# A hybrid decoder layer on one core: SiLU as one ScalarE function, taken for four convolution tiles at a time

## The chip, the core and the metric

The kernel runs on one core of a Trainium2 chip. A core has five engines, each working through its own queue of instructions in order: TensorE (PE; its weight loads are listed as PEld) multiplies matrices, VectorE (DVE) and ScalarE (ACT) work element by element, GpSimd (POOL) does so more slowly, and SyncE (SP) issues most DMAs. Engines wait for each other through semaphores. The metric is the time of one execution on the device in microseconds (us): the median of three runs, and beside it one execution that the hardware profiler recorded.

## The reference, cut to what matters

One layer of a decoder with three token mixers runs over 256 prompt rows and 8 x 4 sample rows, 288 columns in all, in fp32. The part that the change touches is the front of mixer B, a gated delta rule with 4 heads of width 128:

```python
conv = sum(full[:, j:j + L] * conv_w[j] for j in range(CONV_W))      # width 4, per channel
conv = jax.nn.silu(conv).astype(jnp.float32).reshape(n, L, 3, B_HEADS, B_HEAD_DIM)
q = l2_normalize(conv[:, :, 0]) * (B_HEAD_DIM ** -0.5)
k = l2_normalize(conv[:, :, 1])                  # x * rsqrt(sum(x * x) + 1e-6)
v = conv[:, :, 2]
...
o = rms_norm(o, dn_g) * jax.nn.silu(b_z.astype(jnp.float32).reshape(n, L, B_HEADS, B_HEAD_DIM))
```

So 12 channel tiles of 128 (4 of q, 4 of k, 4 of v) are convolved and put through SiLU; q and k are normalised over their 128 channels; four z tiles go through SiLU for the output gate. Around this stand the projections in and out, two attention mixers, the residual norms and an MLP with squared ReLU.

## The kernel before, in words

**Pieces.** All weights come as a list of pieces of 128 x 1024 or 128 x 768, and the main loop in `build` walks through them. A weight is split into a high part (`wh`, a cast on ScalarE, L372) and a low part (`wl`, a subtraction on VectorE, or on GpSimd for a few pieces), the activations likewise (`xh`, `xl`), and each product is three matmuls: high x high, low x high, high x low. A piece of 8 tiles is 24 matmuls, one of 6 tiles is 18. `split_to(i + SA)` with SA = 3 emits the cast of a piece three pieces ahead, into four buffers; `low_to` emits its low part one piece later. Pieces 0 to 88 are the input projection (`w_in`): the attention heads first, then z, a small piece for the gates, and as pieces 65 to 88 the 12 tiles of b, two pieces each. Pieces 89 to 120 are the first output projection (`w_o1`), 121 to 128 the second (`w_o2`), then the MLP.

**Planned side work.** All other work is written as Python generators whose `yield` gives a latency in us of a planning clock `clk`, which counts only estimated TensorE time. Between parts of a piece `advance(BUD)` steps each generator that is ready, in the order of the list, until 1.6 us of planned TensorE work are emitted; `drain(name)` forces a generator to its end. This fixes the order of the instructions in every engine's queue before the program runs; nothing is reordered later.

**The convolution stage.** When both pieces of b tile m are through, `conv_tile(m)` scales the accumulator into `zb` with the rows that precede it, and adds a generator `g_conv(m)` ahead of the others. `g_conv` makes the convolution from one ScalarE and three VectorE instructions (`ca`), then SiLU in parts that need only Exp and Ln: a clamp on VectorE, `silu_e` (Exp, Ln, Exp on ScalarE), `silu_b` (two steps on VectorE, the product on GpSimd). For q and k it goes on: the square (ScalarE), the sum over channels (a matmul with ones), Ln and Exp for a first inverse root `r`, its square, two VectorE steps for the refinement, a product with `r` on GpSimd, and a last product on GpSimd that writes `B["q"]` or `B["k"]` (for the 32 sample columns two small ones into `qD`, `kD`). For v it ends with transposes into `B["vt"]`. Waits in the code keep at most three tiles apart. `g_silu_z` does the same SiLU for the four z tiles when all 12 convolutions are through.

**What follows.** `g_gate` prepares decays early in the stage. `g_chunk(0)` and `g_chunk(1)`, the delta rule of the prompt, poll until the tiles 0 to 7 are done, and need 8 to 11 later; `g_bdec` handles the sample rows and needs the buffers that open when the convolution pool `cv` closes; `g_bfin` applies norm and gate once all are done. The last `w_o1` piece drains `bc0`, `bc1` and `bf`, since `w_o2` reads their result. Later norms (`pre_up`, `g_r2`, the end of the loop) each take Ln and Exp on ScalarE through `rsqrt_a`. At its start the kernel asks for one table of ScalarE functions by name:

```python
S.preload_act_table_set("natural_log_exp_and_others")
```

Helpers record all their uses under one line: `act` is L314, `tt` L317, `ts` L321 and L323, `stt` L326, `mm` L307, `tr` L311.

Of the kernel before, what the change touches and what calls it, by code (L numbers as in the profile page):

```python
# [7 lines left out]
AF = mybir.ActivationFunctionType  # L8
ALU = mybir.AluOpType
# [4 lines left out]
P = 128  # L14
# [3 lines left out]
T = TP + TS  # L18
# [3 lines left out]
EPS = 1e-6  # L22
ZW = 315
CW = 312
# [215 lines left out]
def build(tc, d):  # L240
    nc = tc.nc
    PE, V, S, G, SP = nc.tensor, nc.vector, nc.scalar, nc.gpsimd, nc.sync
# [23 lines left out]
    def mx(n=512, p=P):  # L266
        return ps.t([P, 512], "mx", 4)[0:p, 0:n]
# [6 lines left out]
    ident, ones, tri, triD = (cst[:, k * P:(k + 1) * P] for k in range(4))  # L274
# [10 lines left out]
    dng = pm[:, 112:113]  # L285
# [23 lines left out]
    def tr(out, in_, idn):  # L309
        clk[0] += max(in_.shape[0], in_.free_size()) / 600.0  # L310
        PE.transpose(out, in_, idn)  # L311

    def act(out, in_, func, **kw):
        S.activation(out=out, in_=in_, func=func, **kw)  # L314

    def tt(eng, out, a, b, op):
        eng.tensor_tensor(out=out, in0=a, in1=b, op=op)  # L317

    def ts(eng, out, a, s1, op0, s2=None, op1=None):
        if op1 is None:  # L320
            eng.tensor_scalar(out=out, in0=a, scalar1=s1, scalar2=None, op0=op0)  # L321
        else:
            eng.tensor_scalar(out=out, in0=a, scalar1=s1, scalar2=s2, op0=op0, op1=op1)  # L323

    def stt(eng, out, a, s, b, op0, op1, **kw):
        eng.scalar_tensor_tensor(out=out, in0=a, scalar=s, in1=b, op0=op0, op1=op1, **kw)  # L326
# [23 lines left out]
    LT = (2.8, 2.8, 3.6, 1.4, 1.4, 2.8, 1.4, 1.4, 5.0)  # L350
# [88 lines left out]
    done = set()  # L439

    def add_gen(g, name=None, lat=0.0, front=False):
        at_ = len(gens)
        if front:
            at_ = sum(1 for x in gens if x[1].startswith("conv") and x[1] != "convout")
        gens.insert(at_, (g, name, clk[0] + lat))
# [41 lines left out]
    def drain(*names):  # L487
        guard = 0
        while any(n not in done for n in names):
            for name in [g[1] for g in sorted(gens, key=lambda g: g[2])]:  # L490
                if guard % 6 < 5 and name not in names:
                    continue
                for i in range(len(gens)):
                    if gens[i][1] == name:
                        step(i)
                        break
                if all(n in done for n in names):
                    return
            guard += 1
            assert guard < 5000, (names, [g[1] for g in gens])  # L500
# [8 lines left out]
    mixp = base.t([P, KT, T], "mix")  # L509
# [16 lines left out]
    bp, cv, sp, st = Lazy(), Lazy(), Lazy(), Lazy()  # L526
    cvp = {}
    gate = {}
    B = {}

    def open_b():
        bp.open("b", "right")
        cv.open("cv")
        cvp["buf"] = cv.t([P, 12, 24], "cbuf")
        cvp["co"] = cv.t([P, 12, 27], "convo")
        SP.dma_start(out=cvp["buf"], in_=d["cbuf"])
        B["k"], B["q"] = (bp.t([P, 4, TP], "k4", 2) for _ in range(2))
        B["vt"] = bp.t([P, 2, 4, P], "vt")
        B["kD"], B["qD"], B["vD"] = (bp.t([P, P], t) for t in ("kD", "qD", "vD"))
        B["o"] = bp.t([P, 4, T], "oB")  # L540
        add_gen(g_silu_z(), "siluz", 6.0)
        add_gen(g_gate(), "gate")
        for c in range(2):
            add_gen(g_chunk(c), f"bc{c}")
        add_gen(g_bdec(), "bd")
        add_gen(g_bfin(), "bf")

    def g_silu_z():
        for h in range(4):
            z = mixp[:, 6 + h, :]  # L550
            while not all(f"cs{m}" in done for m in range(12)):
                yield 3.0
            e, q = silu_a(cv, z, T)
            yield 2.0
            silu_e(e, q)
            yield 4.0
            silu_b(e, q, z, G)
            yield 2.5
            act(z, z, AF.Identity, scale=dng)
            yield 1.0  # L560

    def maybe_close_cv():
        if "sp" not in done and all(n in done for n in ["siluz", "gate", "convout"] + [f"conv{m}" for m in range(12)]):
# [2 lines left out]
            sp.open("sp")  # L566
            done.add("sp")

    def silu_a(pool, x, w):
        e = pool.t([P, ZW], "e", 3)  # L570
        s = pool.t([P, ZW], "s", 3)
        ts(V, e[:, :w], x, -80.0, ALU.max)
        return e[:, :w], s[:, :w]

    def silu_e(e, s):
        act(e, e, AF.Exp, scale=-1.0)
        act(s, e, AF.Ln, bias=1.0, scale=1.0)
        act(s, s, AF.Exp, scale=-1.0)

    def silu_b(e, s, x, eng):  # L580
        stt(V, e, e, 1.0, s, ALU.add, ALU.mult)
        stt(V, s, e, 2.0, s, ALU.subtract, ALU.mult, reverse0=True)
        tt(eng, x, x, s, ALU.mult)

    def decv(ap):
        return ap[:, 259:315].rearrange("p (n s) -> p n s", s=7)[:, :, 0:4]

    def conv_tile(m, acc):
        if m >= 4:
            drain(f"conv{m - 4}")  # L590
        if m >= 3:
            drain(f"cz{m - 3}")
        zb = cv.t([P, ZW], "zb", 3)
        G.memset(zb[:, 0:3], 0.0)
        zd = zb[:, 259:315].rearrange("p (n s) -> p n s", s=7)
        G.tensor_copy(out=zd[:, :, 0:3], in_=cvp['buf'][:, m, :].rearrange("p (n s) -> p n s", s=3))
        R = cur["R"]
        tt(V, zb[:, 3:259], acc[:, 0:TP], R[:, 0:TP], ALU.mult)
        tt(V, zd[:, :, 3:7], acc[:, TP:T].rearrange("p (n s) -> p n s", s=4),
           R[:, TP:T].rearrange("p (n s) -> p n s", s=4), ALU.mult)  # L600
        G.tensor_copy(out=cvp['co'][:, m, 0:3], in_=zb[:, 256:259])
        G.tensor_copy(out=cvp['co'][:, m, 3:27].rearrange("p (n s) -> p n s", s=3), in_=zd[:, :, 4:7])
        add_gen(g_conv(m, zb), f"conv{m}", 1.5, front=True)
        if m == 11:
            add_gen(g_convout(), "convout")

    def g_convout():
# [2 lines left out]
            yield 2.0  # L610
        G.dma_start(out=d["conv"], in_=cvp['co'])

    def g_conv(m, zb):
        kind, h = m // 4, m % 4
        while m >= 3 and f"cs{m - 3}" not in done:
            yield 1.0
        y = cv.t([P, ZW], "ca", 5)
        yc = y[:, :CW]
        act(yc, zb[:, 0:CW], AF.Identity, scale=convw[:, m, 0:1])
        yield LT[6]  # L620
        for j in range(1, 4):
            stt(V, yc, zb[:, j:j + CW], convw[:, m, j:j + 1], yc, ALU.mult, ALU.add)
        e = cv.t([P, ZW], "e", 3)[:, :CW]
        q = cv.t([P, ZW], "s", 3)[:, :CW]
        ts(V, e, yc, -80.0, ALU.max)
        done.add(f"cz{m}")
        yield LT[0]
        silu_e(e, q)
        yield LT[1]
        silu_b(e, q, yc, G)  # L630
        done.add(f"cs{m}")
        yield LT[2] if kind < 2 else LT[8]
        if kind < 2:
            while m >= 2 and f"cn{m - 2}" not in done:
                yield 1.0
            sq = cv.t([P, ZW], "sq", 2)
            act(sq[:, :CW], yc, AF.Square)
            yield LT[3]
            p = lx(CW)
            mm(p, ones, sq[:, :CW])  # L640
            yield LT[4]
            r = cv.t([P, CW], "nr", 2)
            act(r, p, AF.Ln, bias=epsc[:, 0:1], scale=1.0)
            act(r, r, AF.Exp, scale=-0.5)
            w = sq[:, :CW]
            act(w, r, AF.Square)
            yield LT[5]
            sc = float(P) ** -0.5 if kind == 0 else 1.0
            stt(V, w, p, EPS, w, ALU.add, ALU.mult)
            ts(V, w, w, -0.5 * sc, ALU.mult, 1.5 * sc, ALU.add)  # L650
            tt(G, yc, yc, r, ALU.mult)
            yield LT[7]
            dp, dd = ((B["q"], B["qD"]), (B["k"], B["kD"]))[kind]
            tt(G, dp[:, h, :], y[:, 0:TP], w[:, 0:TP], ALU.mult)
            yv = decv(y)
            dv_ = dd[:, 32 * h:32 * h + 32].rearrange("p (n s) -> p n s", s=4)
            tt(G, dv_[:, 0:7, :], yv[:, 0:7, :], sq[:, 259:308].rearrange("p (n s) -> p n s", s=7)[:, :, 0:4], ALU.mult)
            tt(G, dv_[:, 7, :], yv[:, 7, :], sq[:, 308:312], ALU.mult)
            done.add(f"cn{m}")
        else:  # L660
            G.tensor_copy(out=B["vD"][:, 32 * h:32 * h + 32].rearrange("p (n s) -> p n s", s=4), in_=decv(y))
            p = mx(256)
            for c in range(2):
                tr(p[:, c * P:(c + 1) * P], y[:, c * P:(c + 1) * P], ident)
            S.copy(out=B["vt"][:, :, h, :], in_=p.rearrange("p (c n) -> p c n", c=2))

    def g_gate():
        pool = bp
# [972 lines left out]
    with tc.manual_schedule():  # L1641
# [90 lines left out]
        p = mx(T)  # L1732
        mm(p, ones, ml["acc"], stop=False)
        mm(p, ones, ml["sql"], start=False)
        t, r = rsqrt_a(ml["p"], p, 1.0 / D, "m")
        newton(V, r, t, p, r, 1.0 / D, EPS)
        y = ml["y"]
# [35 lines left out]
```

## Time and profile before

| | us |
|---|---|
| median of three runs (lowest, highest) | 1449.59 (1447.74, 1450.51) |
| the profiled execution | 1447.53 |
| its span | 1445.8 |
| busy: TensorE, VectorE, ScalarE, GpSimd | 1391.1, 826.5, 605.6, 212.2 |

The span runs from the first to the last instruction; some 2 us of the execution's time lie around it. A group's row names line, engine and operation, output <- inputs with their pool's name (`cv` is the convolution stage's pool, `b` the delta rule's, `sp` the output gate's, `ml` the MLP's, `base` what lives throughout, `ps` the accumulators), partitions x elements, the count, and then the busy time and the mean of one instruction. A timeline row begins with the start and the duration in us, and in brackets stands the idle time of its engine before it with what ended it. TensorE's busy time comes from modelled ends of pipelined matmuls, so the granted clock (PEclk) has to be read beside it.

### The profile page before, as it was taken

What the parts mean: (1) busy time and instruction counts of PE and PEld (TensorE: products, weight loads), DVE (VectorE), ACT (ScalarE), POOL (GpSimd) and SP (SyncE); (2) the same over time, 40 slices, a digit from 0 to 9 for tenths busy, and PEclk for the clock granted to TensorE, in tenths of its full rate; (3) what the DMA queues carried; (4) which work ended last, traced back from release to release, by engine and by line L of the source; (5) the groups of instructions that cost most, each with busy time, mean ns of one, the idle gap of its engine ahead of it and who ended that gap; (6) DMA issues with size and microseconds to landing.
All of it is one profiled execution on the core that took longest, in us unless ns stands there. A gap on an engine that the chain in (4) does not pass through costs nothing.

```text
span 1445.8 us, 25828 instructions
## 1 busy us (share of the span) xinstructions
PE 1391.1 (96%) x10673; PEld 1322.8 (91%) x10673; DVE 826.5 (57%) x1310; ACT 605.6 (42%) x958; POOL 212.2 (15%) x266
## 2 busy tenths in 40 slices
PE   7899999999999999899999999999999999999994
PEld 7788788789889999699999999999999999999994
DVE  7354455547998657895533455544555444555555
ACT  6342434435664236553333334333334333334441
POOL 2112110104851015620000000000000000000114
PEclk9999999999999999999999999999999999999997
DMA  7778888743333335365545445545545545445541
GB/s 265 262 267 321 314 309 337 279 166 124 129 103 104 107 125 168 131 198 181 171 166 168 154 160 175 164 160 172 163 160 174 167 159 171 164 158 174 169 153 65
DMA packets 70629, 262.26 MB, mean 181 GB/s; under 512 B 8080, under 2 KB 10256, under 8 KB 70512
## 3 DMA queue, kind: packets, MB, share of 16 engines
q1 hardware_dynamic: 68112, 254.94, 51.5%
q0 software_dynamic: 1536, 4.89, 0.9%
q8 instruction: 83, 1.36, 0.4%
q10 hardware_dynamic: 864, 0.80, 0.2%
q14 instruction: 34, 0.28, 0.1%
HBM read 253.35 MB, written 7.24 MB: 180 GB/s over the span
## 4 chain that ended last, share of the span: by engine, by line
PE 84%; DVE 9%; issue 2%; ACT 2%; DMA 1%; POOL 1%; SPq 0%; POOLq 0%; DVEq 0%; ACTq 0%
PE ps_mx L307 33%; PE ps_acc L307 31%; PE ps_lx L307 20%; DVE cv_ca L326 2%; DVE base_wl L317 2%; PE ps_mx L311 1%; POOL ml_y L317 1%; DMA kv_kv<-kv_k 1%; DVE base_mix L317 1%; DMA base_wr<-w_in 1%; DVE base_xl L326 1%; ACT base_wh L372 1%; DVE cv_e L326 0%; DVE base_xl L317 0%; DVE ml_sacc L317 0%
## 5 line engine op out<-in xcount | busy, mean ns | idle before, releaser
L372 ACT CAST base_wh<-base_wr 128x1024 fp32r<-128x1024 f32 (+1 forms) x384 | 395.2, 1031 | 579.5 <-PE ps_mx L307 221.9
L317 DVE TENSOR_TENSOR base_wl<-base_wr,base_wh 128x1024 fp32r<-128x1024 f32 (+1 forms) x377 | 462.9, 1242 | 67.1 <-ACT base_wh L372 65.3
L307 PE MATMUL ps_acc<-base_xh,base_wh 128*128 128x288 f32 (+1 forms) x1072 | 331.4, 310 | 5.0 <-ACT base_xh L1449 2.8
L307 PE MATMUL ps_acc<-base_xl,base_wh 128*128 128x288 f32 (+1 forms) x1072 | 321.5, 300 | 3.2 <-DVE base_xl L326 3.1
L307 PE MATMUL ps_acc<-base_xh,base_wl 128*128 128x288 f32 x1056 | 315.1, 298 | 0.6 <-DVE base_wl L317 0.6
L307 PEld LDWEIGHTS ps_acc<-base_xh,base_wh 128*128 128x128 f32 (+1 forms) x1072 | 203.9, 190 | 25.6 <-issue 16.8
L307 PEld LDWEIGHTS ps_acc<-base_xl,base_wh 128*128 128x128 f32 (+1 forms) x1072 | 203.9, 190 | 7.7 <-DVE base_xl L326 6.1
L307 PEld LDWEIGHTS ps_acc<-base_xh,base_wl 128*128 128x128 f32 x1056 | 202.6, 192 | 1.5 <-DVE base_wl L317 1.4
L307 PE MATMUL ps_mx<-ml_big,base_wh 128*128 128x288 f32 x1024 | 203.3, 294 | 0.0
L307 PEld LDWEIGHTS ps_mx<-ml_big,base_wh 128*128 128x128 f32 x1024 | 164.1, 188 | 0.0
L307 PE MATMUL ps_mx<-base_xh,base_wh 128*128 128x288 f32 x512 | 151.7, 296 | 1.1 <-DVE st_s L317 1.1
L307 PE MATMUL ps_mx<-base_xh,base_wl 128*128 128x288 f32 x512 | 150.8, 295 | 0.5 <-DVE base_wl L317 0.4
L307 PE MATMUL ps_mx<-base_xl,base_wh 128*128 128x288 f32 x512 | 151.0, 295 | 0.0
L307 PE MATMUL ps_mx<-ml_big,base_wl 128*128 128x288 f32 x512 | 150.9, 295 | 0.0
L307 PE MATMUL ps_lx<-base_xh,base_wh 128*128 128x288 f32 x416 | 126.0, 303 | 6.3 <-ACT base_xh L314 6.3
L317 POOL TENSOR_TENSOR ml_sacc<-ml_sacc,ml_sq 128x288 f32<-128x288 f32 x20 | 18.3, 913 | 742.9 <-ACT ml_sq L314 742.8
L307 PE MATMUL ps_lx<-base_xh,base_wl 128*128 128x288 f32 x416 | 123.3, 296 | 1.6 <-DVE base_wl L317 1.6
L307 PE MATMUL ps_lx<-base_xl,base_wh 128*128 128x288 f32 x416 | 123.6, 297 | 0.0
L307 PE MATMUL ps_lx<-ml_big,base_wh 128*128 128x288 f32 x512 | 101.8, 294 | 0.0
L307 PE MATMUL ps_acc<-ml_big,base_wh 128*128 128x288 f32 x512 | 101.8, 294 | 0.0
L307 PEld LDWEIGHTS ps_mx<-base_xh,base_wh 128*128 128x128 f32 x512 | 95.9, 187 | 1.7 <-ACT ml_sq L314 1.0
L307 PEld LDWEIGHTS ps_mx<-base_xh,base_wl 128*128 128x128 f32 x512 | 96.4, 188 | 1.0 <-DVE base_wl L317 0.9
(392 smaller groups left out, 1993.8 us busy)
## 6 DMA issues: line engine op xcount, KB each, us to landing
base_wr<-w_up SPq DMA_DIRECT2D x128, 512.0 KB, 3.7
base_wr<-w_dn SPq DMA_DIRECT2D x128, 512.0 KB, 3.4
base_wr<-w_in SPq DMA_DIRECT2D x88, 512.0 KB, 4.4
kv_kv<-kv_k SPq DMA_DIRECT2D x24, 896.0 KB, 8.4
kv_kv<-kv_v SPq DMA_DIRECT2D x28, 768.0 KB, 7.8
base_wr<-w_o SPq DMA_DIRECT2D x32, 384.0 KB, 3.0
base_wr<-w_o SPq DMA_DIRECT2D x8, 512.0 KB, 3.5
ml_big<-xT SPq DMA_DIRECT2D x4, 576.0 KB, 5.4
```

The lines of the kernel that those rows point to most:

```text
L307: PE.matmul(out, lhsT=lhsT, rhs=rhs, start=start, stop=stop, **kw)
L311: PE.transpose(out, in_, idn)
L317: eng.tensor_tensor(out=out, in0=a, in1=b, op=op)
L326: eng.scalar_tensor_tensor(out=out, in0=a, scalar=s, in1=b, op0=op0, op1=op1, **kw)
L372: S.copy(out=p["wh"], in_=p["wr"])
```

## The change

`g_conv` now ends after the convolution itself. The generator `g_group(kind)`, one for q, k and v each, waits until its four tiles are convolved, then emits four ScalarE SiLU instructions in a row. The group of q first also takes SiLU over the four z tiles as one instruction 1152 wide, and scales them with `dng`; `g_silu_z`, `silu_a`, `silu_e` and `silu_b` are gone. After that the group walks through its tiles one by one. The norm's square of `r` on ScalarE and its scale-and-shift on VectorE are replaced by two further VectorE steps that multiply by `r` each time, so that the whole factor is in `w`, and the product with `r` on GpSimd is gone: one product with `w` remains for the prompt columns (and the two small ones). The convolved tiles live in nine buffers where there were five. The names of functions and tables elsewhere are as before.

```diff
-        add_gen(g_silu_z(), "siluz", 6.0)
...
     def conv_tile(m, acc):
-        if m >= 4:
-            drain(f"conv{m - 4}")
+        if m >= NCA:
+            while f"conv{m - NCA}" not in done:
+                drain(f"convg{(m - NCA) // 4}")
...
-        add_gen(g_conv(m, zb), f"conv{m}", 1.5, front=True)
+        add_gen(g_conv(m, zb), f"convt{m}", 1.5, front=True)
+        if m % 4 == 3:
+            add_gen(g_group(m // 4), f"convg{m // 4}", 1.5, front=True)
...
+    NCA = 9
+
     def g_conv(m, zb):
-        kind, h = m // 4, m % 4
-        while m >= 3 and f"cs{m - 3}" not in done:
-            yield 1.0
-        y = cv.t([P, ZW], "ca", 5)
+        y = cv.t([P, ZW], "ca", NCA)
+        cvp["y", m] = y
...
-        e = cv.t([P, ZW], "e", 3)[:, :CW]
-        q = cv.t([P, ZW], "s", 3)[:, :CW]
-        ts(V, e, yc, -80.0, ALU.max)
         done.add(f"cz{m}")
-        yield LT[0]
-        silu_e(e, q)
-        yield LT[1]
-        silu_b(e, q, yc, G)
-        done.add(f"cs{m}")
...
+    def g_group(kind):
+        ms = range(4 * kind, 4 * kind + 4)
+        while not all(f"cz{m}" in done for m in ms):
+            yield 1.0
+        yield 1.5
+        if kind == 0:
+            zs = mixp[:, 6:10, :]
+            act(zs, zs, AF.Silu)
+        for m in ms:
+            yc = cvp["y", m][:, :CW]
+            act(yc, yc, AF.Silu)
+        if kind == 0:
+            act(zs, zs, AF.Identity, scale=dng)
+            done.add("siluz")
+        yield 2.0
+        for m in ms:
+            h = m % 4
+            y = cvp.pop(("y", m))
+            yc = y[:, :CW]
+            if kind == 2:
...
+                done.add(f"conv{m}")
+                yield 0.7
+                continue
             sq = cv.t([P, ZW], "sq", 2)
             act(sq[:, :CW], yc, AF.Square)
-            yield LT[3]
+            yield 1.0
             p = lx(CW)
             mm(p, ones, sq[:, :CW])
-            yield LT[4]
+            yield 1.0
             r = cv.t([P, CW], "nr", 2)
             act(r, p, AF.Ln, bias=epsc[:, 0:1], scale=1.0)
             act(r, r, AF.Exp, scale=-0.5)
             w = sq[:, :CW]
-            act(w, r, AF.Square)
-            yield LT[5]
             sc = float(P) ** -0.5 if kind == 0 else 1.0
-            stt(V, w, p, EPS, w, ALU.add, ALU.mult)
-            ts(V, w, w, -0.5 * sc, ALU.mult, 1.5 * sc, ALU.add)
-            tt(G, yc, yc, r, ALU.mult)
-            yield LT[7]
+            stt(V, w, p, EPS, r, ALU.add, ALU.mult)
+            stt(V, w, w, -0.5 * sc, r, ALU.mult, ALU.mult)
+            stt(V, w, w, 1.5 * sc, r, ALU.add, ALU.mult)
+            yield 2.0
```

More of the change, by code (lines that the diff above doesn't have):

```diff
@@ L546, in open_b @@
         add_gen(g_bfin(), "bf")
[L548 to L554, printed above, removed]
-            silu_e(e, q)
[L556 to L559, printed above, removed]
-            yield 1.0
     def maybe_close_cv():
@@ L567, in maybe_close_cv @@
             done.add("sp")
[L569 to L583, printed above, removed]
     def decv(ap):
@@ L611, in g_convout @@
         G.dma_start(out=d["conv"], in_=cvp['co'])
+    NCA = 9
     def g_conv(m, zb):
-        kind, h = m // 4, m % 4
-        while m >= 3 and f"cs{m - 3}" not in done:
-            yield 1.0
-        y = cv.t([P, ZW], "ca", 5)
+        y = cv.t([P, ZW], "ca", NCA)
+        cvp["y", m] = y
         yc = y[:, :CW]
@@ L622, in g_conv @@
             stt(V, yc, zb[:, j:j + CW], convw[:, m, j:j + 1], yc, ALU.mult, ALU.add)
-        e = cv.t([P, ZW], "e", 3)[:, :CW]
-        q = cv.t([P, ZW], "s", 3)[:, :CW]
-        ts(V, e, yc, -80.0, ALU.max)
         done.add(f"cz{m}")
-        yield LT[0]
-        silu_e(e, q)
-        yield LT[1]
-        silu_b(e, q, yc, G)
-        done.add(f"cs{m}")
[L632 to L635, printed above, removed]
+    def g_group(kind):
[18 more added lines that the diff above has]
+            if kind == 2:
+                G.tensor_copy(out=B["vD"][:, 32 * h:32 * h + 32].rearrange("p (n s) -> p n s", s=4), in_=decv(y))
+                p = mx(256)
+                for c in range(2):
+                    tr(p[:, c * P:(c + 1) * P], y[:, c * P:(c + 1) * P], ident)
+                S.copy(out=B["vt"][:, :, h, :], in_=p.rearrange("p (c n) -> p c n", c=2))
+                done.add(f"conv{m}")
+                yield 0.7
+                continue
             sq = cv.t([P, ZW], "sq", 2)
             act(sq[:, :CW], yc, AF.Square)
-            yield LT[3]
+            yield 1.0
             p = lx(CW)
             mm(p, ones, sq[:, :CW])
-            yield LT[4]
+            yield 1.0
             r = cv.t([P, CW], "nr", 2)
@@ L658, in g_conv @@
             tt(G, dv_[:, 7, :], yv[:, 7, :], sq[:, 308:312], ALU.mult)
[L659 to L665, printed above, removed]
+            done.add(f"conv{m}")
     def g_gate():
```

## The prediction

> **What bounds the kernel now.** First the page: TensorE is busy 96% of the span, so only stretches in which it waits or runs at a lower clock can give time back. The table of stretches (us from the span's start; busy time and instructions of each engine, granted clock, DMA) shows one around the change:
>
> ```profile
> core 0: us, PE busy (x) PEld busy (x) DVE busy (x) ACT busy (x) POOL busy (x), PEclk, DMA share, GB/s
> 330.00:346.00 16.00, 14.57 (x105) 13.60 (x105) 13.55 (x24) 7.96 (x14) 5.92 (x13) 1.00 0.42 140
> 346.00:362.00 16.00, 15.86 (x104) 15.33 (x104) 13.58 (x29) 10.80 (x22) 8.25 (x15) 0.89 0.34 115
> 362.00:423.00 61.00, 55.30 (x392) 53.71 (x391) 59.74 (x90) 42.06 (x82) 48.04 (x69) 0.97 0.35 115
> 423.00:445.00 22.00, 19.88 (x146) 18.24 (x145) 21.62 (x49) 14.23 (x34) 7.24 (x10) 1.00 0.30 98
> ```
>
> From 362 to 423, VectorE is busy 59.7 of 61 us, TensorE 55.3. TensorE's idle time in the four rows is 1.4 + 0.1 + 5.7 + 2.1 = 9.4 us; the clock costs about 0.11 x 15.9 + 0.03 x 55.3 = 3.4 us more. So 12.8 us is the most that this stage can give: 3.3 before 362, 7.4 to 423, 2.1 behind. The chain of waits, cut to this stage, agrees, and the same chain later gives TensorE's own rate, 25.60 / 192 = 0.133 us a matmul:
>
> ```profile
> by line: DVE cv_ca L326 20.3%; DVE base_wl L317 12.2%; PE ps_acc L307 11.8%; issue 8.3%; DVE cv_e L326 5.4%; PE ps_mx L307 4.0%; DVE base_xl L317 3.9%; DVE cv_s L326 3.4%; PE ps_lx L307 3.3%; ACT base_wh L372 3.2%; DVE cv_zb L317 2.9%; ACT
> ...
> 673.24 25.60 PE ps_mx L307 x192
> ```
>
> Two tiles are four weight pieces, 96 matmuls: 12.8 us, and about 1 us for two norm sums: 13.8. What two tiles take now is the step from one row to the next but one of its kind in VectorE's timeline:
>
> ```profile
> 379.23 4.18 DVE L326 SCALAR_TENSOR_TENSOR cv_ca<-cv_zb,base_pm,cv_ca 128x312 f32<-128x312 f32 x3
> ...
> 395.79 4.19 DVE L326 SCALAR_TENSOR_TENSOR cv_ca<-cv_zb,base_pm,cv_ca 128x312 f32<-128x312 f32 x3
> ...
> 412.35 2.18 DVE L326 SCALAR_TENSOR_TENSOR cv_ca<-cv_zb,base_pm,cv_ca 128x312 f32<-128x312 f32 x3
> ...
> 430.98 1.70 DVE L326 SCALAR_TENSOR_TENSOR cv_ca<-cv_zb,base_pm,cv_ca 128x312 f32<-128x312 f32 x3
> ```
>
> That is 16.56 us for a pair. The same three instructions take 1.70 us where GpSimd is quiet, 2.18 beside one GpSimd product and 4.19 beside GpSimd's low part of a weight piece: GpSimd's work costs VectorE time.
>
> **The change, part by part.** The groups of instructions between 330 and 445 (x count | busy us, mean ns):
>
> ```profile
> L372 ACT CAST base_wh<-base_wr 128x1024 fp32r<-128x1024 f32 (+1 forms) x29 | 28.1, 968 | 9.5 <-PE ps_acc L307 9.5
> L326 DVE SCALAR_TENSOR_TENSOR cv_e<-cv_e,cv_s 128x312 f32<-128x312 f32 x12 | 9.5, 791 | 0.0
> L323 DVE TENSOR_SCALAR cv_sq<-cv_sq 128x312 f32<-128x312 f32 x8 | 6.5, 810 | 0.3
> L314 ACT ACTIVATE cv_s<-cv_s 128x312 f32<-128x312 f32 (+1 forms) x13 | 6.0, 463 | 0.4
> L326 DVE SCALAR_TENSOR_TENSOR cv_s<-cv_e,cv_s 128x312 f32<-128x312 f32 x12 | 5.8, 484 | 0.4
> L321 DVE TENSOR_SCALAR cv_e<-cv_ca 128x312 f32<-128x312 f32 x12 | 3.9, 323 | 0.4
> L326 DVE SCALAR_TENSOR_TENSOR cv_sq<-ps_lx,cv_sq 128x312 f32<-128x312 f32 x8 | 3.8, 474 | 0.0
> L314 ACT ACTIVATE cv_nr<-ps_lx,base_epsc 128x312 f32<-128x312 f32 x8 | 4.1, 513 | 0.0
> L314 ACT ACTIVATE cv_sq<-cv_nr 128x312 f32<-128x312 f32 x8 | 3.7, 466 | 0.3
> ```
>
> VectorE, for a pair of tiles: removed are the clamp, the two SiLU steps and the scale-and-shift, 2 x (0.323 + 0.791 + 0.484 + 0.810) = 4.8 us, and the stall beside GpSimd's SiLU product, 2 x 0.48 = 1.0; added are two more scalar-tensor-tensors a tile, 4 x 0.474 = 1.9. The remaining GpSimd product will push something else by about 0.5 a tile, 1.0. 16.56 - 5.8 + 1.9 + 1.0 = 13.7 us. VectorE alone would then no longer bind; TensorE's 13.8 would, and nearly all of the 7.4 us would come back.
>
> ScalarE, for a pair: now 42.06 / 61 x 16.56 = 11.4 us. Away go three functions of the SiLU and the square of the factor, 2 x (3 x 0.463 + 0.466) = 3.7; one function comes, 2 x 0.463 = 0.9. That leaves 8.6 us, but the function tables are not in it. The whole run before has one load of them:
>
> ```profile
> L1642 ACT ACT_TABLE_LOAD  x1: 1283/1283/1283, 0.7 to 0.7; - x1
> ...
> 4.62 1.04 ACT L372 CAST base_wh<-base_wr 128x1024 fp32r<-128x1024 f32 x1 [2.60 <-DMA base_wr<-w_in]
> ```
>
> The kernel asks for it by name, for the set natural_log_exp_and_others, and Exp, Ln, Square and Identity all run on it. No row shows SiLU, so its loads are bounded from both sides: none, if that set held it, or one at each change between SiLU, Ln and Exp. I take the second: the new code names no set after the first SiLU, and a load placed for Ln alone, in front of Ln alone, need not bring Exp with it. Then each of the two normalised groups has 1 + 4 x 2 = 9 loads, the third 1, the delta rule's first Exp 1, and each later Ln and Exp pair (output gate, two norms of the MLP, the last norm) 2: 28 loads, 28 x 1.283 = 36 us of ScalarE. A switch costs at least 1.283; behind the one load stand 2.60 us of idle time, so at most 3.88; but a DMA ended that idle time, so I take 1.283.
>
> A pair with two norms then has 8.6 + 4 x 1.283 + half a SiLU switch (0.6) = 14.3 us of ScalarE. The planner spaces the norms of a group by 4.0 of its own us plus rounding to its calls, about 5.6, and the tiles by 6.3, so a group's norms come 1.13 times as dense: about 15. ScalarE becomes the bound, with VectorE (13.7, and now waiting in order for each Exp) and TensorE (13.8) right behind it. I take 15.6 for a pair; between 15 and 16.6 lie gains of 5.7 and 0. 61 / 16.56 = 3.7 pairs x 0.95 = **3.5 us gained** from 362 to 423.
>
> Before 362 the pieces that were late are mostly these:
>
> ```profile
> 343.11 1.75 POOL L317 TENSOR_TENSOR cv_ca<-cv_ca,cv_s 128x312 f32<-128x312 f32 x1 [0.54 <-DVE cv_s L326]
> ...
> 345.40 0.38 PE L307 MATMUL ps_mx<-base_cst,cv_bD 8*128 8x8 f32 x2 [1.43 <-POOL cv_bD L693]
> ```
>
> TensorE waits for a copy queued on GpSimd behind the SiLU product, and the clock drops behind the wait (0.89). The product is gone, the first group's SiLU comes only after tile 3: **3 us gained** of 3.3 (0 if another wait steps in).
>
> From 423 to 445: in the old order the norms ended with the win stage; now the last two tiles' Ln and Exp (2 x 3.5 us of ScalarE) and the third SiLU switch fall beside the twelve casts of the mixer's output and the weight casts. **1 us lost** (2 gained to 4 lost). The z tiles' SiLU, moved from 441-497 into group 0, costs ScalarE 2 x 1.17 us there (a 1152 wide instruction, row below) and frees a stretch in which TensorE was full anyway: nothing, covered by the weight casts' lead of three pieces (9.6 us); without it, those 2.3 us.
>
> Behind the stage, the chunk generators start when tile 7 is done. Its yields after the tile add to 19.1 before and 22.4 now, and there are more of them to round up, and the calls thin out at the stage's end: about 3 pieces of the 32 of the first output projection later. Its end, the output gate, already comes late:
>
> ```profile
> 537.91 1.17 ACT L314 ACTIVATE sp_fa<-b_oB 128x1152 f32<-128x1152 f32 x1
> ...
> 547.14 1.19 ACT L314 ACTIVATE sp_fb<-sp_fb 128x1152 f32<-128x1152 f32 x1
> ...
> 550.71 1.68 DVE L326 SCALAR_TENSOR_TENSOR sp_ft<-sp_ft,sp_fa 128x1152 f32<-128x1152 f32 x1
> ...
> 556.08 1.34 DVE L317 TENSOR_TENSOR base_mix<-base_mix,sp_ft 128x1152 f32<-128x1152 f32 x1
> ...
> 557.94 0.61 PE L307 MATMUL ps_acc<-base_xh,base_wh 128*128 128x288 f32 x1 [2.85 <-ACT base_xh L1449]
> ```
>
> It takes 20 us from its square to TensorE's restart. Its own work is about 13: these rows with the step between the VectorE ones (1.8), a second 1.2 on ScalarE, a cast of 0.4, and some 4 for four sums and their evacuations. So 7 us are slack, of which I count 2 as weight casts that stay in between. Starting 3 pieces (3 x 18 x 0.133 = 7.2 us) later it loses 7.2 - 5 = 2.2 us, and the load ahead of its Exp 1.3: **3.5 us lost** (2 gained to 6 lost). The later norms sit bare on the path:
>
> ```profile
> 587.37 1.03 ACT L372 CAST base_wh<-base_wr 128x1024 fp32r<-128x1024 f32 x1
> 588.66 0.50 ACT L314 ACTIVATE ml_m_r<-ps_mx,base_epsc 128x288 f32<-128x288 f32 x1 [0.26 <-PE ps_mx L307]
> ...
> 1426.08 0.54 ACT L314 ACTIVATE ml_y<-ml_y,base_pm 128x288 f32<-128x288 f32 x1
> 1426.89 0.50 ACT L314 ACTIVATE ml_m_r<-ps_mx,base_epsc 128x288 f32<-128x288 f32 x1 [0.27 <-PE ps_mx L307]
> ```
>
> ScalarE is free at 588.40 and Ln starts at 588.66: a load in front delays it by 1.0, the load for Exp by 1.3; at the end likewise 0.9 + 1.3. With 0.4 for the norm between, **4.9 us lost**.
>
> Sum: 3 + 3.5 - 1 - 3.5 - 4.9 = 2.9 us slower than the profiled 1447.53; on the median of 1449.59, which lies 2.1 above it, and with half a microsecond for instructions that no longer overlap across a load: **1453 us**.
>
> By the Trainium skill, "ScalarE: Activation LUTs", What ACT_TABLE_LOAD costs, a switch costs the 1283 ns of this trace's row and a drain of about 1380 ns, 2.66 us in all. By that figure the estimate is the second rival's time. No run here shows it yet.
>
> **The rivals.** (1) After the SiLU one set serves Ln and Exp again. Then a group has two switches, 6 loads in all and none later: ScalarE has 8.6 + 1.3 us for a pair, TensorE binds; 3 + 6.5 gained, 1 lost at the stage's end, 2.2 at the gate: **1443**. For it: one load served both before. Against: that one was asked for by name. By the skill's "ScalarE activation tables", Table sets in the compiler and the runtime, loads are placed for the longest run, which gives this rival.
> (2) A switch costs about twice its load, 2.6 us. A pair then has 15 + 4.5 x 1.3 = 21 us of ScalarE: 3.7 x 4.4 = 16 lost where 3.5 was gained, some 4 more to 445, 6 at the later norms: 1453 + 30 = **1483**. For it: the idle time behind the only load; against: the DMA that ended it.
> (3) Loads as forecast, but ScalarE runs ahead and hides them in the stage, since TensorE waits there for nothing but VectorE: 7 gained of 7.4, the end of the stage even; 3 + 7 - 3.5 - 4.9 = 1.6 gained: **1448**. It decides from the point at which a pair costs ScalarE under 13.8 us.
>
> **How the numbers follow.** Forecast 0.62, its own range 1446 to 1460; (1) 0.13; (2) 0.12; (3) 0.13. A measurement of this kernel tells about 0.2%, 2.9 us, from no change. The forecast alone is slower 0.53, the same 0.35, faster 0.12; (1) is faster 0.85; (2) slower; (3) faster 0.45, same 0.5. Together faster 0.24, same 0.30, slower 0.46. The range of 1443 to 1467 leaves out (2) and the outer ends of the rest.
>
> **What would show it.** Right: 29 table loads, in Ln and Exp pairs; ScalarE over 90% busy between tiles 4 and 11, a pair near 15.6 us; TensorE's wait at 345 gone; each later norm 2.2 us longer; a longer wait at the first weight of the second output projection. Wrong: about 7 loads and a pair of 14 us (1); pairs over 20 us with idle time behind each load (2); pairs at 14 us in spite of 29 loads (3). A stage with no TensorE idle time before 445 would show that the chunk work's later start mattered more than the loads.

## The result

| | before | after |
|---|---|---|
| median (lowest, highest), us | 1449.25 (1447.74, 1450.51) | 1464.03 (1460.20, 1464.65) |
| ratio to before | | 1.010 (95% interval 1.0087 to 1.0112) |
| span of the profiled execution | 1445.8 | 1462.8 |
| busy: TensorE, VectorE, ScalarE, GpSimd | 1391.1, 826.5, 605.6, 212.2 | 1395.0, 800.5, 622.3, 183.0 |

The kernel became 15 us slower. The sign of the forecast holds, and 1464.03 lies in the range of 1443 to 1467; but it lies above the forecast's own range of 1446 to 1460, and the size does not hold, since 3.4 us were forecast. One of the ten executions of the new norm alone, below, took 1532.19 us at a granted clock of 0.842, and it is left out of that kernel's ratio.

The table of stretches of the changed kernel (us from the span's start; busy time and instructions of each engine, granted clock, DMA), for the stretches that the prediction shows of before:

```profile
core 0: us, PE busy (x) PEld busy (x) DVE busy (x) ACT busy (x) POOL busy (x), PEclk, DMA share, GB/s
330.00:346.00 16.00, 16.00 (x119) 15.16 (x117) 11.84 (x22) 6.21 (x10) 6.60 (x12) 1.00 0.38 120
346.00:362.00 16.00, 16.00 (x123) 16.00 (x123) 12.77 (x23) 9.56 (x15) 7.04 (x12) 1.00 0.47 154
362.00:423.00 61.00, 51.10 (x341) 48.33 (x339) 36.23 (x61) 47.10 (x63) 24.63 (x48) 0.94 0.34 111
423.00:445.00 22.00, 18.29 (x119) 17.06 (x120) 18.35 (x40) 18.55 (x38) 6.48 (x12) 0.84 0.24 73
```

Up to 362 TensorE no longer waits and its clock is full. Behind it, VectorE falls from 59.7 to 36.2 us of 61, GpSimd from 48.0 to 24.6, and ScalarE reaches 47.1, 77%. TensorE falls too, from 55.3 to 51.1, 84%. No engine is full. From 330 to 445 TensorE issues 119 + 123 + 341 + 119 = 702 matmuls where it issued 747: 45 x 0.133 = 6 us behind.

ScalarE's groups over the whole run, table loads alone (count | busy us, mean ns | idle before):

```profile
L314 ACT ACT_TABLE_LOAD x28 | 35.9, 1283 | 0.5
...
L1623 ACT ACT_TABLE_LOAD x1 | 1.3, 1283 | 0.7 <-PEq L1744 0.7
```

The 28 loads of the forecast are there, each as long as the one of before. ScalarE's timeline shows where they fall (start, duration; in brackets the idle time before and what ended it):

```profile
394.36 1.28 ACT L314 ACT_TABLE_LOAD   x1
395.66 1.17 ACT L314 ACTIVATE cv_ca<-cv_ca 128x312 f32<-128x312 f32 x3
399.12 0.46 ACT L314 ACTIVATE cv_ca<-cv_ca 128x312 f32<-128x312 f32 x1 [2.30 <-DVE cv_ca L326]
399.49 1.03 ACT L372 CAST base_wh<-base_wr 128x1024 fp32r<-128x1024 f32 x1
400.43 0.46 ACT L314 ACTIVATE cv_sq<-cv_ca 128x312 f32<-128x312 f32 x1
...
402.29 1.28 ACT L314 ACT_TABLE_LOAD   x1
403.58 0.52 ACT L314 ACTIVATE cv_nr<-ps_lx,base_epsc 128x312 f32<-128x312 f32 x1
404.12 1.28 ACT L314 ACT_TABLE_LOAD   x1
405.41 0.46 ACT L314 ACTIVATE cv_nr<-cv_nr 128x312 f32<-128x312 f32 x1
...
442.39 1.28 ACT L314 ACT_TABLE_LOAD   x1
443.68 1.28 ACT L314 ACTIVATE b_cA<-b_cA,b_ngc 128x128 f32<-128x128 f32 x4
```

The second group's SiLU burst waits in ScalarE's queue 2.3 us for the last of its four convolutions, and the square of tile 4 stands behind it and a weight cast. Then the norms of tiles 4 to 7 follow one another, each with a load ahead of Ln and one ahead of Exp, and only behind tile 7, the third burst and one more load comes the first Exp of the delta rule (`b_cA`), at 443.68. In the kernel before:

```profile
429.51 1.26 ACT L314 ACTIVATE b_cA<-b_cA,b_ngc 128x128 f32<-128x128 f32 x4
```

TensorE's longest waits between 330 and 650 in the changed kernel (us in total, times, longest):

```profile
PE ps_acc L307 <- ACT base_xh L1430: 9.4, 2, 7.1
PE ps_lx L307 <- ACT cv_sq L314: 8.4, 4, 6.3
```

And its timeline at the output gate, first ScalarE's square, then TensorE's first matmul behind the gate:

```profile
549.50 1.17 ACT L314 ACTIVATE sp_fa<-b_oB 128x1152 f32<-128x1152 f32 x1
...
569.02 0.61 PE L307 MATMUL ps_acc<-base_xh,base_wh 128*128 128x288 f32 x1 [7.13 <-ACT base_xh L1430]
```

The longest of the `cv_sq` waits, 6.3 us, is the sum of tile 4 waiting for the square above. The longest of all, 7.1 us, stands at the gate: its square comes at 549.50 instead of 537.91, and TensorE restarts at 569.02 instead of 557.94. The delta rule starts 14.2 us later, the gate comes 11.6 later, TensorE's restart 11.1.

Part of this lies ahead of the change. VectorE's first convolution steps, those of tile 0, in the kernel before and in the changed one:

```profile
337.35 1.70 DVE L326 SCALAR_TENSOR_TENSOR cv_ca<-cv_zb,base_pm,cv_ca 128x312 f32<-128x312 f32 x3 [0.56 <-ACT cv_ca L314]
...
339.14 1.70 DVE L326 SCALAR_TENSOR_TENSOR cv_ca<-cv_zb,base_pm,cv_ca 128x312 f32<-128x312 f32 x3 [0.56 <-ACT cv_ca L314]
```

None of the changed instructions stands ahead of this one, and two kernels below that are alike up to here (the set named in each group, and named last) reach it 2.0 us apart. So instants of two kernels are better compared from this step on. Counted so, the first Exp comes 12.4 us later, the gate's square 9.8, TensorE's restart 9.3.

### The profile page after: what moved, and what is told of

Read it like the earlier page. It is cut to its first block, busy times and chain, and to the rows that moved or that the text cites. A ratio compares the mean times of both kernels' runs of the same rounds, so it can differ in the third digit from the quotient of the medians.

```text
span 1462.8 us, 25757 instructions
## 1 busy us (share of the span) xinstructions
PE 1395.0 (95%) x10673; PEld 1324.3 (91%) x10673; DVE 800.5 (55%) x1270; ACT 622.3 (43%) x940; POOL 183.0 (13%) x242
## 4 chain that ended last, share of the span: by engine, by line
PE 64%; DVE 3%; POOL 2%; ACT 1%; issue 1%; POOLq 0%; DVEq 0%; ACTq 0%
PE ps_mx L307 31%; PE ps_lx L307 17%; PE ps_acc L307 16%; POOL ml_y L317 1%; DVE base_mix L317 1%; POOL base_R L317 1%; DVE base_xl L326 0%; ACT L314 0%; DVE ml_sacc L317 0%; DVE base_wl L317 0%; DVE base_oext L317 0%; DVE sp_ft L326 0%; PE ps_mx L311 0%; ACT sp_fb L314 0%; ACT base_wh L372 0%
## 5 line engine op out<-in xcount | busy, mean ns | idle before, releaser
L317 DVE TENSOR_TENSOR base_wl<-base_wr,base_wh 128x1024 fp32r<-128x1024 f32 (+1 forms) x377 | 460.6, 1236 | 72.1 <-ACT base_wh L372 68.5
L307 PEld LDWEIGHTS ps_acc<-base_xh,base_wh 128*128 128x128 f32 (+1 forms) x1072 | 204.0, 190 | 33.1 <-issue 17.6
```

What stands on the lines that cost most here:

```text
L307: PE.matmul(out, lhsT=lhsT, rhs=rhs, start=start, stop=stop, **kw)
```

## The experiments

Three theories were open. L: the table loads make the loss. O: the order makes it, since the groups queue much behind each SiLU burst. And, from the second set of runs on, C: what counts is how late the delta rule starts, because the gate follows its first Exp one for one, whatever delays it. None of the kernels below leaves work out.

**The named set behind each burst.** The changed kernel with one line more, so that Ln and Exp find the set that holds both:

```diff
             done.add("siluz")
+        S.preload_act_table_set("natural_log_exp_and_others")
         yield 2.0
```

> The changed kernel, with the set that has both Ln and Exp asked for by name right behind each group's SiLU instructions: 7 loads in all instead of 29. Theory L (the loads and what queues behind them cost the time): ScalarE needs some 10 us for a pair of tiles, TensorE binds again; 1445 us, within 3, so faster than before. Theory O (the later start of the chunk work, an effect of the grouping's order alone, costs most of it): only the loads at the later norms and at the output gate are saved, about 6 us; 1457 us, with the long wait ahead of the second output projection still there.

Measured: 1447.77 us, 0.9994 of before (0.9984 to 1.0004). ScalarE's groups, the loads but for the one at the start:

```profile
L314 ACT ACT_TABLE_LOAD x3 | 3.8, 1283 | 0.1
L611 ACT ACT_TABLE_LOAD x3 | 3.8, 1283 | 0.1
```

The timeline at the points shown above:

```profile
432.13 1.28 ACT L314 ACTIVATE b_cA<-b_cA,b_ngc 128x128 f32<-128x128 f32 x4
...
539.31 1.17 ACT L314 ACTIVATE sp_fa<-b_oB 128x1152 f32<-128x1152 f32 x1
...
557.45 0.61 PE L307 MATMUL ps_acc<-base_xh,base_wh 128*128 128x288 f32 x1 [5.76 <-ACT base_xh L1431]
```

Six loads in place of 28, the same order of work, and the whole loss is gone: L holds, O's 1457 does not. But nothing is won either, in a kernel that frees VectorE. The stretches say where the gain went:

```profile
362.00:423.00 61.00, 54.82 (x368) 52.26 (x366) 45.85 (x82) 38.41 (x67) 23.35 (x49) 0.94 0.35 112
423.00:445.00 22.00, 21.92 (x176) 21.92 (x177) 18.32 (x39) 15.62 (x35) 9.23 (x15) 1.00 0.43 132
```

With 119 and 122 matmuls in the two stretches ahead, TensorE issues 785 from 330 to 445, 38 or 5 us more than before. But counted from the first convolution the first Exp is 0.8 us later than before and the gate's square only 0.4 earlier. So the matmuls done ahead of time are handed back: TensorE waits 5.8 us at the gate (2.85 before), and from its restart to the row `ml_y<-ml_y,base_pm` of the last norm it takes 870.6 us (868.1 before).

**The named set only behind the last burst**, which takes the loads of the later stages away and leaves those of the stage:

```diff
             done.add("siluz")
+        if kind == 2:
+            S.preload_act_table_set("natural_log_exp_and_others")
         yield 2.0
```

> The changed kernel, with the set asked for by name only behind the third group's SiLU: the loads in the convolution stage stay (19 of them), those of the output gate, the MLP norms and the last norm go. Both theories: 2.2 us each at two later norms and 1.3 us at the gate, so 1458 us. It parts the loads of the stage from the later ones: under theory L the step from here to the run with a named set in each group is over 10 us, under theory O under 3 us.

Measured: 1456.93, 1.006 (1.0045 to 1.0075).

ScalarE's timeline:

```profile
441.47 1.28 ACT L314 ACTIVATE b_cA<-b_cA,b_ngc 128x128 f32<-128x128 f32 x4
...
547.28 1.17 ACT L314 ACTIVATE sp_fa<-b_oB 128x1152 f32<-128x1152 f32 x1
```

So the loads of the stage cost 1456.93 - 1447.77 = 9.2 us, near the 10 that L wanted and far over O's 3. Counted from the first convolution (337.18 here, 339.18 with the set named in each group), the first Exp is 11.3 us later and the gate's square 10.0. The two kernels differ by 14 loads, 18.0 us of ScalarE. The loads behind the stage are the step to the changed kernel, 1464.03 - 1456.93 = 7.1.

**The new norm alone**, in the kernel before with its own SiLU, and the reverse: the groups with the named set and the norm of before.

```diff
-            act(w, r, AF.Square)
...
-            stt(V, w, p, EPS, w, ALU.add, ALU.mult)
-            ts(V, w, w, -0.5 * sc, ALU.mult, 1.5 * sc, ALU.add)
-            tt(G, yc, yc, r, ALU.mult)
+            stt(V, w, p, EPS, r, ALU.add, ALU.mult)
+            stt(V, w, w, -0.5 * sc, r, ALU.mult, ALU.mult)
+            stt(V, w, w, 1.5 * sc, r, ALU.add, ALU.mult)
```

> The kernel before with the new norm alone (three VectorE steps that use the factor directly, no square of the factor on ScalarE, one GpSimd product less); SiLU and its order as before. VectorE by its rows: 0.810 us of scale-and-shift replaced by 2 x 0.474 a tile, and some 0.5 us less beside the GpSimd product: 0.4 us a tile gained on eight tiles, so 1447 us; if the GpSimd product cost VectorE nothing, 1450 to 1451 us.

> SiLU in groups as in the change and the table set named again behind each group, one tile at a time (1447.77), but the norm of before: square of the factor on ScalarE, one scalar-tensor-tensor and one scale-and-shift on VectorE, two GpSimd products. If the new norm is what costs here, as alone in the kernel before (2.6 us slower): 1445. If the prediction's VectorE sum is right, where the new norm frees 0.5 us of VectorE for a pair plus the stall beside the GpSimd product: 1449 to 1451. If the norm is not on the chain: 1447.8.

Measured: 1451.24 for the new norm alone, 1.0017 (1.0008 to 1.0027), and 1448.20 for the groups with the old norm, 1.000 (0.9991 to 1.0009). The stretch of the new norm alone:

```profile
362.00:423.00 61.00, 52.89 (x384) 51.32 (x383) 59.54 (x94) 37.91 (x72) 43.72 (x65) 1.00 0.37 119
```

That is the dearer of the two cases, in which the product on GpSimd costs VectorE nothing: VectorE stays at 59.5 of 61 us, and from 330 to 445 its convolution steps take 33.1 us with the product and without it. The norm sheds 6.5 us of scale-and-shift there and adds 7.7 of new steps, so the relief of VectorE seen above comes from SiLU. Under the groups the two norms differ by 0.4 us; the norm is no part of the loss.

**The delta rule late, and nothing else.** The kernel before, without any of the change:

```diff
         while "gate" not in done or not all(f"conv{m}" in done for m in range(8)):
             yield 3.0
+        yield 10.0
```

> The kernel before, with nothing of the change, but the first step of both chunks of the delta rule put 10 of the planner's own us later. Theory C: the gate's end follows the first Exp of the delta rule one for one, so with that Exp 10 to 13 us later (429.5 becomes about 441) the whole is 9 to 13 us later: 1460, plus or minus 3. Theory of the prediction, 5 us of slack ahead of the first weight of the second output projection: 5 to 8 us later, 1455. If TensorE is full anyway and the order of its work does not matter: 1449.

Measured: 1458.31, 1.007 (1.0055 to 1.0086), which is 9.7 us.

Its timeline at the same points:

```profile
439.59 1.28 ACT L314 ACTIVATE b_cA<-b_cA,b_ngc 128x128 f32<-128x128 f32 x4
...
548.69 1.17 ACT L314 ACTIVATE sp_fa<-b_oB 128x1152 f32<-128x1152 f32 x1
...
564.78 0.61 PE L307 MATMUL ps_acc<-base_xh,base_wh 128*128 128x288 f32 x1 [8.51 <-ACT base_xh L1450]
```

The first Exp is 10.1 us later, the gate's square 10.8, the end 9.7 by the medians (12.8 in the profiled executions, counted from the first convolution): about one for one, in a kernel without a SiLU group or a table load behind the start. Some slack does exist between square and restart (16.1 us instead of 20.0), but it is lost again soon: in the 5 us behind the restart the granted clock is 0.50, where before shows 0.68, and TensorE then waits 4.6 us once for `base_R`, where before it waited 1.5. Why `base_R` comes late was not tried.

**The norms two tiles at a time.** Both squares, both sums, Ln twice, Exp twice, then VectorE and GpSimd; once with the named set, once without:

```diff
-        for m in ms:
+        for pair in (ms[0:2], ms[2:4]):
...
+            for w_ in W:
+                r = cv.t([P, CW], "nr", 2)
+                act(r, w_[3], AF.Ln, bias=epsc[:, 0:1], scale=1.0)
+                w_.append(r)
+            for w_ in W:
+                act(w_[4], w_[4], AF.Exp, scale=-0.5)
```

> As the run with a named set in each group, and the norms of a group taken two tiles at a time, so that the planned time from the last k tile to the start of the chunk work is shorter by half of a group's yields (about 8 planned us, 3 pieces). Theory L: a group's order matters little, within 2 us of the run with a named set in each group. Theory O: the wait ahead of the second output projection falls back to the 3 us that it was before, and the time is 8 us or more below the run with a named set in each group.

> The changed kernel with its norms two tiles at a time and no table set named: both Ln, then both Exp, so 20 extra loads instead of 28, with the order of the pairs kernel that names its set (1442.66). Theory C, the loads count as delay on the chain from the norms of tiles 4 to 7 to the first Exp of the delta rule, and the gate's end follows that Exp: some 7 loads more ahead of that Exp than in the kernel that names its set, at 0.8 us each (11.6 us for 14 in the two kernels without pairs) 6 us, and the 6.7 us of loads behind the stage: 1455, plus or minus 3, the first Exp near 426. Theory of the prediction, loads count only where ScalarE's pair of tiles rises over TensorE's 13.8 us: 8.6 + 2.5 loads of 1.283 + 0.6 is 12.4, nothing lost in the stage, and only the loads behind it: 1449, the first Exp near 420.

Measured with the set named: 1442.66, 0.9957 (0.9943 to 0.9972), 5 us under the same kernel tile by tile. ScalarE's timeline there:

```profile
405.07 0.46 ACT L314 ACTIVATE cv_sq<-cv_ca 128x312 f32<-128x312 f32 x1 [4.02 <-POOL b_kD L317]
...
420.38 1.28 ACT L314 ACTIVATE b_cA<-b_cA,b_ngc 128x128 f32<-128x128 f32 x4
```

The first Exp moves 11.7 us ahead of the kernel tile by tile, 8.1 counted from the first convolution; the expectation had only L and O in it, and 5 us lies between them. TensorE's wait for `base_xh` at the gate falls from 5.8 to 1.3 us, so an earlier start alone could bring little more. Without the set, with 20 loads in all (one fewer than expected, since the first Exp now comes ahead of the third burst and finds its set): 1454.08, 1.0042 (1.0028 to 1.0055); the forecast by C was 1455 with the Exp near 426, that by the prediction's own rule 1449 near 420. The Exp came here, in ScalarE's timeline,

```profile
427.42 1.28 ACT L314 ACTIVATE b_cA<-b_cA,b_ngc 128x128 f32<-128x128 f32 x4
```

5.3 us behind the kernel that names its set, counted from the first convolution, so C is borne out where the two differ.

**More buffers for the square.** The 4.0 us of wait above is that of a square for its buffer, which GpSimd's products of the pair before still read; these stand behind a copy that waits 8.6 us for VectorE's scaling of a convolution input (`cv_zb`).

```diff
-                sq = cv.t([P, ZW], "sq", 2)
+                sq = cv.t([P, ZW], "sq", 4)
```

> The pairs kernel that names its set (1442.66), with four buffers for the square and the norm factor instead of two. There TensorE stands 2.3 us at 405 for a square that waits 4.0 us for GpSimd's products of the pair before, which stand behind a copy of a convolution input that waits for TensorE. Theory C: that wait goes, the first Exp comes 2 to 4 us earlier than 420.4, and the end with it: 1439.5, plus or minus 1.5. Rival: the planner's own spacing sets where the sum stands, and another wait steps in: 1442.7.

Measured: 1436.66, 0.992 (0.9907 to 0.9934). TensorE's wait for squares between 330 and 650 was 7.8 us in six waits with two buffers; now the waits have

```profile
PE ps_lx L307 <- ACT cv_sq L314: 3.6, 2, 2.3
```

and ScalarE's timeline

```profile
416.93 1.27 ACT L314 ACTIVATE b_cA<-b_cA,b_ngc 128x128 f32<-128x128 f32 x4
...
519.18 0.59 ACT L862 COPY b_oB<-ps_mx 128x512 f32<-128x512 f32 x1 [3.26 <-PE ps_mx L307]
...
527.07 1.17 ACT L314 ACTIVATE sp_fa<-b_oB 128x1152 f32<-128x1152 f32 x1
```

The wait goes, the first Exp is 3.5 us earlier, and the time falls by 6.0, more than C's 3. Counted from the first convolution (335.52 with two buffers, 337.46 here) the Exp is 5.4 us earlier and the gate's square 4.7. TensorE comes earlier by itself too, since its waits for squares fall by 4.2; its wait at the gate stays at 1.3. This kernel beats both of the case: 0.8% under before, where the changed one is 1.0% over.

**Groups of two tiles**, for tiles 0 to 7 and for 4 to 7 alone, on top of that:

```diff
+    GR = ([0, 1], [2, 3], [4, 5], [6, 7], [8, 9, 10, 11])
...
-    def g_group(kind):
-        ms = range(4 * kind, 4 * kind + 4)
+    def g_group(ms):
+        kind = ms[0] // 4
```

> The pairs kernel with four buffers (1436.66), with SiLU also in groups of two tiles for the first eight (4 groups, the last four tiles in one): two SiLU switches more, 4 loads more, 5.1 us of ScalarE. Tile 7's norm no longer stands behind those of tiles 4 and 5: the first Exp of the delta rule near 409 instead of 416.9. Theory C one for one: 1429. But TensorE waits only 2.3 us at the gate's end by now, so I expect the gain to stop there: 2 to 5 us, 1433. If the loads in the stage cost more than the earlier start brings: 1438 or more.

> The same with groups of two for tiles 4 to 7 alone; tiles 0 to 3 stay one group: 2 loads more than the kernel with four buffers (1436.66). Theory C: the first Exp depends on tiles 4 to 7 alone, so it comes as early as with groups of two throughout, and the time is within 2 us of that kernel: 1433. If the first group of four holds TensorE up (its 2.3 us of wait near 363), it is 2 us slower than that one.

Measured: 1440.30 (0.9945, 0.9931 to 0.9960) and 1442.75 (0.9958, 0.9943 to 0.9972), both slower than with groups of four. The 2.5 us between the two are not clear, since their executions overlap (1438.46 to 1441.75 and 1440.28 to 1443.15), so whether the first group of four holds TensorE up stays open. In the second the first Exp comes at 404.98, as early as in the first. ScalarE's timeline in the first:

```profile
405.15 1.28 ACT L314 ACTIVATE b_cA<-b_cA,b_ngc 128x128 f32<-128x128 f32 x4
...
514.99 0.59 ACT L864 COPY b_oB<-ps_mx 128x512 f32<-128x512 f32 x1 [2.49 <-PE ps_mx L307]
527.40 0.27 ACT L945 COPY b_oB<-ps_mx 128x128 f32<-128x128 f32 x1 [2.46 <-PE ps_mx L307]
527.70 1.17 ACT L314 ACTIVATE sp_fa<-b_oB 128x1152 f32<-128x1152 f32 x1
```

The Exp is 11.8 us earlier still and the gate's square not at all. This is C's limit, and the rows show what waits. The delta rule of the prompt does follow the Exp in part: its second copy into `b_oB` comes at 514.99 instead of 519.18. But the gate's square stands behind the copy of the sample rows, which comes at 527.40 (526.77 with groups of four). In all the kernels above this copy starts 3.2 or 7.6 us behind the prompt's, here 12.4. The sample rows' generator, `g_bdec`, needs all twelve tiles, and its first product on VectorE (`b_dB`) comes at 452.8 here and at 438.4 with groups of four. A kernel that starts the sample rows earlier was not tried, and why the time is 3.6 us longer with the square nearly in place is open. Both times miss the 1433 that was expected; they lie where the loads in the stage would cost more than the earlier start brings, but no run here shows that cause.

The points side by side, in us (before: the runs beside the later kernels). The instants are those of one profiled execution each; the last column but one takes out what lies ahead of the stage:

| kernel | loads | first convolution | first Exp | gate's square | first Exp to square | first convolution to square | median |
|---|---|---|---|---|---|---|---|
| before | 1 | 337.4 | 429.5 | 537.9 | 108.4 | 200.6 | 1448.6 |
| new norm alone | 1 | 337.2 | 432.3 | 540.8 | 108.4 | 203.5 | 1451.2 |
| delta rule late | 1 | 337.0 | 439.6 | 548.7 | 109.1 | 211.7 | 1458.3 |
| changed | 29 | 339.1 | 443.7 | 549.5 | 105.8 | 210.4 | 1464.0 |
| set named last | 21 | 337.2 | 441.5 | 547.3 | 105.8 | 210.1 | 1456.9 |
| set named | 7 | 339.2 | 432.1 | 539.3 | 107.2 | 200.1 | 1447.8 |
| set named, old norm | 7 | 336.9 | 430.0 | 536.9 | 106.9 | 200.0 | 1448.2 |
| pairs | 20 | 337.3 | 427.4 | 537.5 | 110.1 | 200.2 | 1454.1 |
| pairs, set named | 7 | 335.5 | 420.4 | 529.8 | 109.4 | 194.3 | 1442.7 |
| pairs, set named, four buffers | 7 | 337.5 | 416.9 | 527.1 | 110.1 | 189.6 | 1436.7 |
| the same, groups of two | 11 | 337.5 | 405.2 | 527.7 | 122.6 | 190.2 | 1440.3 |
| the same, groups of two for 4 to 7 | 9 | 336.1 | 405.0 | 527.5 | 122.6 | 191.5 | 1442.8 |

From the first Exp to the square it is 106 to 110 us in all kernels but the last two. And in the kernels without a load behind the stage, these two left out, the median follows the last column but one: each differs from before in both by the same, within 1.4 us, from 11 us less (four buffers) to 11 us more (delta rule late). The changed kernel and the pairs without a named set lie 5.6 and 5.9 us above that, which is another measure of the loads behind the stage.

## Why the prediction was right, and where its size was wrong

| term of the sum | forecast | measured |
|---|---|---|
| edits with six loads, those of the first rival (3 + 6.5 gained, 1 + 2.2 lost) | -6.3 | -0.9 (set named, against before) |
| loads in the stage (3.5 gained in place of 6.5) | +3.0 | +9.2 (set named last, against set named) |
| loads behind it (1.3 + 4.9, and 0.5) | +6.7 | +7.1 (changed, against set named last) |
| sum | +3.4 | +15.4 (+14.8 against its own runs of before) |

**The loads: right.** 28 more, 1.283 us each, in pairs for Ln and Exp. The load at 404.12 ends at 405.40 and Exp starts at 405.41, and ScalarE's idle time ahead of all 28 is 0.5 us together, so no drain lies on either side and the second rival falls; its figure of 2.66 us a switch, from the Trainium skill, "ScalarE: Activation LUTs", What ACT_TABLE_LOAD costs, isn't seen in this trace. The first rival, one set for Ln and Exp, did not happen of itself; the longest run of the Trainium skill, "ScalarE activation tables: per-element evaluation and per-set limits", Table sets in the compiler and the runtime, would have given it, and the 28 loads say otherwise. It does happen as soon as the set is named, with six loads, but then it gives 1447.8 and not 1443.

**Behind the stage: right in its sum, in part by luck.** The last norm has both loads on the path, in ScalarE's timeline:

```profile
1440.51 0.54 ACT L314 ACTIVATE ml_y<-ml_y,base_pm 128x288 f32<-128x288 f32 x1
1441.06 1.28 ACT L314 ACT_TABLE_LOAD   x1
1442.35 0.50 ACT L314 ACTIVATE ml_m_r<-ps_mx,base_epsc 128x288 f32<-128x288 f32 x1
1442.87 1.28 ACT L314 ACT_TABLE_LOAD   x1
```

They make it 2.2 us longer, as forecast. The gate takes 1.4 us more than with the set named last (square to restart 19.5 against 18.1), where 1.3 was forecast. But the first norm of the MLP hides the load for Ln:

```profile
599.53 1.28 ACT L314 ACT_TABLE_LOAD   x1
601.77 0.50 ACT L314 ACTIVATE ml_m_r<-ps_mx,base_epsc 128x288 f32<-128x288 f32 x1 [0.96 <-PE ps_mx L307]
```

The load is done 0.96 us before TensorE's sum, which waited 2.6 us for GpSimd's `base_R` (1.5 before). The two norms of the MLP together cost 0.9 us (871.5 against 870.6 from the restart to the last norm), not the 2.7 of the sum. So the rows show 4.5 of the 6.7 that were forecast. The medians lie 7.1 apart; the two profiled executions lie 6.8 apart, and 2.0 of these stand ahead of the first convolution.

**Before 362: right.** 3.3 us were to be had by busy time and clock, and both stretches are full now at a clock of 1.00. By the counted matmuls, 242 where there were 209, it is a little more: 33 x 0.133 = 4.4 us. The wait for the GpSimd copy is gone.

**From 362 to 423: wrong.** "ScalarE becomes the bound" at 15.6 us a pair, over 90% busy. ScalarE is 77% busy, and a pair takes longer all the same. The prediction's 16.56 us holds between tiles 5 and 9; over two whole groups, from the convolution of tile 3 to that of tile 11, VectorE's timeline has, first before (its end is the row at 430.98 above), then changed:

```profile
362.53 4.34 DVE L326 SCALAR_TENSOR_TENSOR cv_ca<-cv_zb,base_pm,cv_ca 128x312 f32<-128x312 f32 x3
...
358.72 3.85 DVE L326 SCALAR_TENSOR_TENSOR cv_ca<-cv_zb,base_pm,cv_ca 128x312 f32<-128x312 f32 x3
...
438.40 1.62 DVE L326 SCALAR_TENSOR_TENSOR cv_ca<-cv_zb,base_pm,cv_ca 128x312 f32<-128x312 f32 x2
```

That is 68.5 us before, 17.1 a pair, and 79.7 after, 19.9 a pair. ScalarE's work for a pair was sized well, 47.10 / 61 x 19.9 = 15.4 us. But even with the set named the way is 67.9 us, 17.0 a pair and no shorter than before, though ScalarE is then busy 38.4 of 61 us and VectorE 45.9. The sum took each engine's work for a pair and let the largest bind. That held before, when VectorE was full. After, no engine is: each norm is a round through ScalarE, TensorE, ScalarE, VectorE and GpSimd, one tile behind the other. That this round is the limit is borne out by the pairs: with two tiles to a round and the same loads and functions, the first Exp is 8.1 us earlier. And a load in the round counts as time on an engine with 23% to spare: of the 18.0 us of the 14 loads, 11.3 reach the first Exp.

**423 to 445 and the gate: wrong, and the larger part.** The step that failed reads: "Starting 3 pieces (3 x 18 x 0.133 = 7.2 us) later it loses 7.2 - 5 = 2.2 us". By the sum's own gains, 3 + 3.5 - 1 = 5.5 us by then, this Exp would have come some 2 us later. It came 14.2 us later, 12.4 counted from the first convolution: 0.8 from the order (set named, against before) and 11.6 from the loads (changed, against set named). For loads that delay this Exp the sum had nothing; it counted those of the stage only where they fill ScalarE. And the slack of 5 was worth little: counted the same way, the gate's square moved by 9.8 and TensorE's restart by 9.3. The run with the late delta rule shows 3.9 us of such slack, and shows it lost again behind the gate. The prediction had the right mechanism here, the delta rule's start, but as a side cost of 3.5 us beside a gain of TensorE's own; in fact the gate's square follows this start, and what TensorE gains in the stage comes back as idle time at the gate and behind it. Hence -0.9 in place of -6.3, and 9.2 in place of 3.0. The sign came out right because the loads cost more than the edits gain, as forecast, but both terms missed to the same side, so that the range held by only 3 us. What the z tiles' SiLU costs in the first group was not tried alone.

**The third rival**, loads hidden in the stage, fell for the same reason: ScalarE had room, and the loads were not hidden. Of the marks that were named, the pairs of loads, the vanished wait at 345 and the longer wait at the first weight of the second output projection came true (7.1 us after 2.85); ScalarE over 90% and a pair near 15.6 us did not, and "each later norm 2.2 us longer" holds for the last norm alone.

## What to carry to other kernels

Where an engine's work falls and nothing gets faster, look in the timeline for the instruction that starts the next serial stage: here the first Exp of the delta rule tells when the output gate comes, within a few microseconds until another branch is the last to arrive, while the busy shares tell nothing. Instants of two profiled executions are compared from a common point right ahead of the change, since the executions can differ by microseconds before it. A table load in a round trip between engines costs most of its length even if ScalarE is a quarter idle, and none where the engine would have waited anyway; so a set is named again behind each use of a function from another, and functions of one set are gathered over as many tiles as the buffers allow, with a buffer for each tile in flight. A gain ahead of a join is only worth as much as the branch that arrives last is moved.

## What the runs showed of the hardware

A table load took 1283 ns in each of the 28 cases, with the next function 0.01 to 0.02 us behind it unless that one waited for TensorE's sum, and a load placed for Ln did not serve the Exp that followed: two loads for each such pair, none once the set that holds both was named. ScalarE's idle time ahead of the 28 loads was 0.5 us in all. The granted clock falls behind TensorE's waits: in the 5 us behind the restart at the gate it was 1.00 after a wait of 1.3 us (the three kernels with pairs and groups of four), 0.68 and 0.50 after waits of 2.8 (before, and the new norm alone), and 0.50 to 0.54 after 5.8 to 8.5 (five kernels). So here a wait of 2.8 us or more costs more than its own length.
